# Four changes of order in a two-layer hybrid decoder trunk: pooling units swapped, state additions moved ahead of the norm, decays and an epsilon moved

## The chip, the cores and the metric

The kernel runs on one core of one Trainium2 chip. The metric is the device time of one execution in microseconds, as the median of several runs. All arithmetic is float32; large matrix products are made of two parts per operand (a high and a low one), in three passes.

## The reference, cut to what matters

A sequence of 2048 tokens with 1024 channels runs through two layers. Layer 0 has one input projection that feeds gated linear attention (4 heads, chunks of 64, with a low-rank, data-dependent forget gate) and a spatial-gating MLP. Layer 1 has one input projection that feeds retention (4 heads, rotary positions) and a causal pooling mixer of widths 2, 4, 8 and 16. In both layers each branch is multiplied by a SiLU gate, the branches are concatenated and projected back, and x becomes LayerNorm(alpha * x + y). The parts that the change touches:

```python
# layer 0, the forget gate
log_a = log_sigmoid(a_lr @ w_a2 + b_a) / 16          # a_lr: 16 columns of the input projection
b = cumsum(log_a)  # within chunks of 64
q_dec, k_dec = q * exp(b), k * exp(-b)
...
# both layers, chunkwise: state entering each chunk
S[n] = decay[n-1] * S[n-1] + U[n-1]
o = o_intra + q_dec @ S
o_a = rmsnorm(o) * silu(g_a)         # layer 1: groupnorm(o) * silu(g_c)
...
# layer 1, pooling: group g of 128 channels has width w = (2, 4, 8, 16)[g]
outs[g] = mean of the last w tokens - p[g]
o_d = (outs[g] @ w_pool[g]) * scale * silu(g_d)
...
y = concat([o_c, o_d]) @ w_out
x = layer_norm(alpha * x + y)                        # (x - mu) * rsqrt(var + eps) * g + b
```

## The kernel before, in words

**Tiling and order.** The 2048 tokens are worked in 4 blocks of 512; each block goes through both layers before the next. Every projection is a *unit* (`unit`, L164): 512 output columns or rows, as 4 tiles of 128, each summed over 8 k-tiles in 3 passes of a 128x512 matmul on TensorE. With `width=2` a unit is two halves of two tiles, 48 matmuls per half. The order of instructions is written by hand: each engine runs its own in the order in which the program issues them. There is no planner.

**Steps.** What isn't a projection is cut into steps that are put between chunks of a unit. `later(fn, delay)` (L144) appends a step; `between()` (L147) counts each step's delay down by one and runs those that reach zero, in the order in which they were appended. With `width=2`, `between()` is called in the middle of each half (after 4 of 8 k-tiles) and after the half's results have been handed to `evac`: four times a unit. A step that `evac` appends with a delay of 1 runs in the same half's closing `between()`. `flush()` (L158) runs everything that is left.

**Weights.** They stream in 256 KB loads on SP's queue (`fetch`, L102) in the order of `stream`, whose groups follow `ORDER` (L33), into a ring of 7 raw buffers. `cut` (L114) splits one into a high part (a ScalarE copy, L89) and a low part (a VectorE subtraction, L90) in a ring of 12 slots. `pace` (L124) issues cuts while a unit runs, as slots come free: eight in each second half, in steady state.

**PSUM.** Projections take 4 banks (`big`), attention 2 (`att`, L389), and transposes, chunk states, pooling products and decay products share 2 banks (`tr`, L77, tile name `trp`).

**Layer 0's gate.** The first unit of a layer gives half of the values and the 16 low-rank columns. `low_rank` transposes these (L511) into `alrT` (L512), `decay` calls `gla_decay` (products L455; Abs, Exp and Ln on ScalarE, L458 to L464), and `decay2` calls `gla_exps` (cumulative sum on VectorE, L471 to L478; exponentials on ScalarE, L482 to L485). They are steps of the second values unit, whose chunks are half as long (256 columns). The unit of queries and keys follows; when its first half ends, `evac_qk` multiplies by the exponentials into G (L549, L550), and `state_keys` transposes G two steps later (L555).

**Attention.** `attend` (L378) serves both layers. It appends `first` and four `outputs(t)`, one per tile of 128 tokens. `outputs(t)` issues the output products of tile t (L385, into the two `att` banks), then the scores and the chunk states of tile t+1 (into both `tr` banks), then `norm` (statistics, and the POOL's `rstd`), then `prepare` of tile t+1 (masked copies of the scores, L413; four state additions, L417, which read the `tr` banks; the state's decay, L733 in layer 1), and last the scaling, L752 in layer 1, which frees the `att` banks.

**Layer 1's units.** They are, in this order: queries and keys, values, `pool_unit(1)` (widths 8 and 16), the gates of retention, `pool_unit(0)` (widths 2 and 4), and then the output projection with its layer norm. The delays (3, 4, 5, 7, 9) put `first` in the middle of the second half of the values unit, outputs(0) at its end, outputs(1) and outputs(2) in the middles of the two halves of the first pooling unit, and outputs(3) in the middle of the first half of the unit behind it. A pooling unit's first half gives two groups of p: copies into `pb` (L786), then `sums`: shifted additions on VectorE (L793; 1, 2, 3 and 4 of them for widths 2, 4, 8 and 16), a small POOL correction in block 0 alone (L796), the mean minus identity (L798) and the split into `cd`. Its second half gives two SiLU gates (L773), and then `out` multiplies by the pooling weights (products L778, 3 per group, into a `tr` bank) and by the gate (`gate`, L206), whose result is split into the same place of `cd` (L207). `slot = (g + 2) % 4` places the groups, so the output projection takes widths 8 and 16 as k-tiles 4 and 5 and widths 2 and 4 as 6 and 7.

**Layer norm.** `layer_norm_out` (L209) adds the residual (L219), takes statistics (L220, L223), lets `rstd` (L192) form (var + eps) ** -0.5 on the POOL in two instructions (L198 the sum, L201 the power), while the VectorE runs the first normalising pass (L228); the second pass (L231) waits for the POOL. `rstd` with a float epsilon and a scale of 1 is used here and in layer 0's spatial gating (L608).

Of the kernel before, what the change touches and what calls it, by code (L numbers as in the profile page):

```python
# [13 lines left out]
ALU = mybir.AluOpType  # L14
# [15 lines left out]
SLOTS = 12  # L30


ORDER = [0, 1, 2, 3, 4, 5, 6, 7, 8, 11, 9, 10, 12, 13]  # L33


def _parts(value, bits, n):
# [15 lines left out]
def trunk(ctx, tc, x, xT, pos, wv, w, w_a2, pvec, rowp, sgu_rows, w_sT, w_pool, ropec, poolc, out):  # L52
    nc = tc.nc
# [23 lines left out]
    def tr():  # L77
        return ps_tr.tile([P, 4, P], F32, tag="tr", name="trp")

    def w2(name):  # L80
        return work.tile([P, TB], F32, tag="w2", name=name)

    def flat(t):
        return t.rearrange("p a b -> p (a b)")


    def split(src, hi, lo):

        nc.scalar.activation(hi, src, AF.Copy)  # L89
        nc.vector.tensor_tensor(lo, src, hi.bitcast(F32), op=ALU.subtract)  # L90
# [4 lines left out]
    for b in range(NB):  # L95
        stream += [(wv[kt, :, 0:272],) for kt in range(KT)]
        stream += [(wv[kt, :, 272:528], wv[kt + 1, :, 272:528]) for kt in range(0, KT, 2)]
        stream += [(w[g, kt],) for g in ORDER for kt in range(KT)]
    landed, ready, small_loads = [], [], []
# [44 lines left out]
    def later(fn, delay=1):  # L144
        steps.append([delay, fn])
# [12 lines left out]
    def flush():  # L158
        while steps:
            between()  # L160
# [31 lines left out]
    def rstd(dst, var, eps, scale=1.0):  # L192

        n = dst.shape[1]
        if not isinstance(eps, float):
            nc.gpsimd.tensor_tensor(dst, var, eps, op=ALU.add)
        elif scale == 1.0:
            nc.gpsimd.tensor_scalar(dst, var, eps, None, op0=ALU.add)  # L198
        else:
            nc.gpsimd.tensor_scalar(dst, var, scale, eps, op0=ALU.mult, op1=ALU.add)  # L200
        nc.gpsimd.tensor_tensor(dst, dst, neghalf[:, :n], op=ALU.pow)  # L201

    def gate(dst_u, h, psT, gain, sil):

        y = w2("y")
        nc.vector.scalar_tensor_tensor(y, psT, gain, sil, op0=ALU.mult, op1=ALU.mult)  # L206
        later(lambda: split(y, dst_u[:, h, 0, :], dst_u[:, h, 1, :]))  # L207
# [55 lines left out]
    s_mid = const.tile([P, 2, P], F32, name="s_mid")  # L263
# [24 lines left out]
    for kt in range(KT):  # L288
# [4 lines left out]
        t = wpool.tile([P, 2, 512], F32R, tag="w", name="wt")  # L293
# [64 lines left out]
    def half(n):  # L358
        return slice(64 * n, 64 * n + 64)
# [18 lines left out]
    def attend(qk, kt, vt, state, upd, norm, delays):  # L378

        states = [state, s_odd]

        def mm(dst, lhsT, rhs, start=False, stop=False):
            nc.tensor.matmul(dst, lhsT=lhsT, rhs=rhs, start=start, stop=stop, skip_group_check=True)  # L385

        def banks():

            return [ps_s.tile([P, 4, P], F32, tag="s", name="att") for _ in range(2)]  # L389

        def vals(t, s, r, c):
            return vt(t)[half(r), (2 * c + s) * P:(2 * c + s + 1) * P]

        def scores(t, ps, start):
            for c in range(2):
                for s in range(2):
                    for r in range(2):
                        k, q = qk(s, 64 * r, t)
                        mm(ps[r][half(r), 2 + c, half(s)], k[:, half(c)], q[:, half(c)],
                           start=start and c == 0 and s == 0, stop=True)  # L400

        def chunk_states(t):
            u = [tr(), tr()]
            for s in range(2):
                for c in range(2):
                    for r in range(2):
                        mm(u[r][half(c), s, :], kt(s, r, c, t), vals(t, s, r, c), start=s == 0, stop=True)
            return u

        def prepare(t, ps, u):  # L410
            after = states[(t + 1) % 2]
            for r in range(2):
                nc.vector.copy_predicated(pm[t % 2][half(r)], mask_b[half(r)],  # L413
                                          ps[r][half(r), 2:4, :].rearrange("p c (s i) -> p (c s) i", i=64))
            for dst, src, c in ((s_mid, states[t % 2], 0), (after, s_mid, 1)):
                for r in range(2):
                    nc.vector.tensor_tensor(dst[half(r)], src[half(r)], u[r][half(c), 0:2, :], op=ALU.add)  # L417
            upd(t, after)

        def first():  # L420
            ps = banks()
            scores(0, ps, True)
            prepare(0, ps, chunk_states(0))

        def outputs(t):
            m, ps = pm[t % 2], banks()
            last = t == NT - 1
            for s in range(2):
                for c in range(2):
                    for r in range(2):  # L430
                        mm(ps[r][half(c), s, :], m[half(r), 2 * c + s, :], vals(t, s, r, c), start=s == 0)
            for s in range(2):
                for c in range(2):
                    for r in range(2):
                        mm(ps[r][half(c), s, :], qk(s, 64 * r, t)[1][:, half(c)],
                           (states[t % 2], s_mid)[c][half(r), s, :], stop=True)
            if not last:
                scores(t + 1, ps, False)
                u = chunk_states(t + 1)
            scale = norm(t, [p_[:, 0:2, :] for p_ in ps])  # L440
            if not last:
                prepare(t + 1, ps, u)
            scale()

        later(first, delays[0])
        for t in range(NT):
            later(lambda t=t: outputs(t), delays[t + 1])
# [40 lines left out]
    def layer0(b, xs):  # L488
# [6 lines left out]
        def values(t, ps, s):  # L495
            by_heads(both_copy if b == 0 and s == 0 else act_copy,
                     lambda r, c: vt[half(r), t, (2 * c + s) * P:(2 * c + s + 1) * P],
                     lambda c, r: ps[half(c), r * P:(r + 1) * P])
# [31 lines left out]
            later(constants2, 3)  # L530
            later(constants3, 4)
        later(low_rank, 2)
        later(decay, 3)
        later(decay2, 4)
        unit(xs, lambda t, ps: values(t, ps, 1), True, cols=256)


# [124 lines left out]
        for i in range(2):  # L662
            r = r8.tile([P, 2, D], F32, tag="r8", name="rows")
# [23 lines left out]
    def layer1(b, xs, rows):  # L687
# [44 lines left out]
        def upd(t, st):  # L732
            nc.vector.tensor_tensor(st, st, g128.unsqueeze(2).broadcast_to([P, 2, P]), op=ALU.mult)  # L733
# [33 lines left out]
        def pool_unit(half):  # L767
            def evac(n, ps):
                g = 2 * half + n % 2
                slot = (g + 2) % 4  # L770
                if n >= 2:
                    sg = w2("sg")
                    nc.scalar.activation(sg, ps, AF.Silu)  # L773

                    def out():
                        pt = flat(tr())
                        for n, (i, j) in enumerate(PASSES):
                            nc.tensor.matmul(pt, lhsT=wp[:, i, g * P:(g + 1) * P], rhs=cd[:, slot, j, :],  # L778
                                             start=(n == 0), stop=(n == 2))
                        gate(cd, slot, pt, pool_s[:, g:g + 1], sg)  # L780

                    later(out, 1)
                    return
                pb = pl.tile([P, 16 + TB], F32, tag="pl", name="pb")
                nc.vector.tensor_copy(pb[:, 0:16], carry[:, g, :])
                nc.scalar.activation(pb[:, 16:], ps, AF.Copy)  # L786

                def sums():
                    src, off, step = pb, 0, 1
                    while step < WINDOWS[g]:  # L790
                        off2 = off + step
                        dst = pl.tile([P, 16 + TB], F32, tag="pl", name="pl")
                        nc.vector.tensor_tensor(dst[:, off2:], src[:, off2:], src[:, off2 - step:16 + TB - step], op=ALU.add)  # L793
                        src, off, step = dst, off2, step * 2
                    if b == 0:
                        nc.gpsimd.tensor_tensor(src[:, 16:32], src[:, 16:32], poolt[:, g, :], op=ALU.mult)  # L796
                    pd = w2("pd")
                    nc.vector.scalar_tensor_tensor(pd, src[:, 16:], 1.0 / WINDOWS[g], pb[:, 16:],  # L798
                                                   op0=ALU.mult, op1=ALU.subtract)
                    if b < NB - 1:  # L800
                        nc.vector.tensor_copy(carry[:, g, :], pb[:, TB:TB + 16])

                    split(pd, cd[:, slot, 0, :], cd[:, slot, 1, :])

                later(sums)

            unit(xs, evac, False)

        pool_unit(1)

        def evac_gc(h, ps):
            sg = w2("sg")
# [8 lines left out]
            later(out, 1)  # L821

        unit(xs, evac_gc, False)
        pool_unit(0)
        flush()
        load_x(b + 1)

# [21 lines left out]
    for b in range(NB):  # L849
        x1, rows = layer0(b, list(xunits))  # L850
        layer1(b, x1, rows)
# [68 lines left out]
```

## Time and profile before

| | |
|---|---|
| median of 3 runs | 1496.98 us (1495.4 to 1497.81) |
| the profiled execution's own time | 1497.93 us |
| its span, from the first to the last instruction | 1496.2 us |
| TensorE matmuls | 1468.6 us busy (98%), 8752 of them |
| VectorE | 983.5 us (66%) |
| ScalarE (ACT) | 596.3 us (40%) |
| GpSimd (POOL) | 115.9 us (8%) |
| mean granted TensorE clock | 0.994 of full speed |
| DMA | 162.35 MB, mean 109 GB/s |

PE is TensorE's matmuls and PEld its weight loads, DVE is VectorE, ACT is ScalarE, POOL is GpSimd, SP issues the DMAs. The time lies 1.7 us above the span, for what stands around it. Matmuls are pipelined, so that the busy share of TensorE says little of how near it is to its peak; its waits and its granted clock say where time is lost. Idle time of the other engines costs nothing unless TensorE, or the end of the program, waits for them.

### The profile page before, as it was taken

What the parts mean: (1) busy time and instruction counts of PE and PEld (TensorE: products, weight loads), DVE (VectorE), ACT (ScalarE), POOL (GpSimd) and SP (SyncE); (2) the same over time, 40 slices, a digit from 0 to 9 for tenths busy, and PEclk for the clock granted to TensorE, in tenths of its full rate; (3) what the DMA queues carried; (4) which work ended last, traced back from release to release, by engine and by line L of the source; (5) the groups of instructions that cost most, each with busy time, mean ns of one, the idle gap of its engine ahead of it and who ended that gap; (6) DMA issues with size and microseconds to landing.
All of it is one profiled execution on the core that took longest, in us unless ns stands there. A gap on an engine that the chain in (4) does not pass through costs nothing.

```text
span 1496.2 us, 23299 instructions
## 1 busy us (share of the span) xinstructions
PE 1468.6 (98%) x8752; PEld 1225.9 (82%) x8752; DVE 983.5 (66%) x2008; ACT 596.3 (40%) x1116; POOL 115.9 (8%) x185
## 2 busy tenths in 40 slices
PE   8999999999999999999999999999999999999997
PEld 7788888788988888878898888887888888888786
DVE  5596586756657458676665746867576664696755
ACT  6534324243653333434274342333427434143430
POOL 1020010000101001000100100000010010100002
PEclk9999999999999999999999999999999999999999
DMA  7324423124523341313452343232435325222321
GB/s 231 106 85 141 134 64 114 57 67 161 184 71 108 120 141 57 114 57 110 131 183 78 93 139 115 59 111 64 144 103 171 92 79 170 84 92 79 97 80 57
DMA packets 87058, 162.35 MB, mean 109 GB/s; under 512 B 10096, under 2 KB 18336, under 8 KB 86944
## 3 DMA queue, kind: packets, MB, share of 16 engines
q1 hardware_dynamic: 86944, 160.85, 34.6%
q8 instruction: 69, 1.13, 0.3%
q14 instruction: 45, 0.37, 0.1%
HBM read 152.43 MB, written 8.39 MB: 107 GB/s over the span
## 4 chain that ended last, share of the span: by engine, by line
PE 93%; DVE 4%; ACT 1%; DMA 1%; issue 1%; POOL 0%; DVEq 0%; POOLq 0%; ACTq 0%; SPq 0%
PE big L181 84%; PE att L385 3%; DVE pl L793 1%; PE trp L778 1%; PE trp L626 1%; PE trp L678 1%; PE trp L385 1%; DVE wt L90 1%; PE trp L818 0%; PE trp L653 0%; PE trp L718 0%; DMA raw<-in_wv 0%; DMA xraw<-in_xT 0%; ACT T L89 0%; DVE pd L798 0%
## 5 line engine op out<-in xcount | busy, mean ns | idle before, releaser
L181 PE MATMUL big<-wt,T 128*128 128x512 f32 (+2 forms) x3456 | 726.0, 369 | 7.2 <-ACT wt L89 4.5
L181 PEld LDWEIGHTS big<-wt,T 128*128 128x128 f32 x3456 | 599.0, 189 | 114.2 <-ACT wt L89 4.5
L181 PE MATMUL big<-T,wt 128*128 128x512 f32 x2688 | 629.7, 393 | 0.8 <-ACT wt L89 0.8
L181 PEld LDWEIGHTS big<-T,wt 128*128 128x128 f32 x2688 | 502.4, 189 | 109.5 <-issue 4.8
L90 DVE TENSOR_TENSOR wt<-raw,wt 128x512 fp32r<-128x512 f32 (+1 forms) x496 | 317.3, 672 | 247.5 <-ACT wt L89 246.9
L89 ACT ACTIVATE wt<-raw 128x512 fp32r<-128x512 f32 (+1 forms) x496 | 296.7, 616 | 329.0 <-PE big L181 256.4
L219 DVE SCALAR_TENSOR_TENSOR rows<-rows,big 128x512 f32<-128x512 f32 x64 | 43.6, 681 | 59.3 <-PE big L181 59.3
L198 POOL TENSOR_SCALAR lnrs<-lnmv 128x1 f32<-128x1 f32 x32 | 33.3, 1042 | 616.1 <-DVE lnmv L223 616.1
L370 ACT ACTIVATE v<-big 64x128 f32<-64x128 f32 (+1 forms) x184 | 56.7, 308 | 36.0 <-PE big L181 19.0
L680 ACT ACTIVATE T<-trp 128x512 fp32r<-128x512 f32 x32 | 17.4, 596 | 105.7 <-PE trp L678 105.7
L231 DVE SCALAR_TENSOR_TENSOR rows<-rows,lnrs,ln 128x1024 f32<-128x1024 f32 (+1 forms) x36 | 41.6, 1166 | 19.5 <-POOL lnrs L201 18.6
L201 POOL TENSOR_TENSOR rs<-rs,neghalf 128x4 f32<-128x4 f32 x48 | 49.3, 1028 | 3.9
L220 DVE BATCH_NORM_STATS2 lnst<-rows 128x6 f32<-128x512 f32 x64 | 44.4, 694 | 2.2
L228 DVE SCALAR_TENSOR_TENSOR rows<-rows,lnmv,ln 128x1024 f32<-128x1024 f32 x32 | 41.0, 1282 | 0.9
L206 DVE SCALAR_TENSOR_TENSOR y<-trp,pv,sg 128x512 f32<-128x512 f32 x48 | 33.7, 744 | 9.5 <-PE trp L653 5.3
L786 ACT ACTIVATE pb<-big 128x512 f32<-128x512 f32 x16 | 9.6, 598 | 75.0 <-PE big L181 74.5
L638 ACT ACTIVATE act<-big 128x512 f32<-128x512 f32 x32 | 18.3, 597 | 51.2 <-PE big L181 50.5
L89 ACT ACTIVATE T<-y 128x512 fp32r<-128x512 f32 x48 | 29.4, 627 | 22.2 <-DVE y L206 21.8
L604 DVE BATCH_NORM_STATS2 st<-zt 128x6 f32<-128x128 f32 x64 | 13.7, 276 | 35.1 <-ACT zt L600 35.1
L90 DVE TENSOR_TENSOR T<-y,T 128x512 fp32r<-128x512 f32 x48 | 31.7, 689 | 0.5
L793 DVE TENSOR_TENSOR pl<-pb 128x527 f32<-128x527 f32 x16 | 11.3, 704 | 31.2 <-ACT pb L786 31.2
L744 DVE BATCH_NORM_STATS2 st<-att 128x6 f32<-128x128 f32 x64 | 14.2, 284 | 22.5 <-PE att L385 22.0
(197 smaller groups left out, 978.6 us busy)
## 6 DMA issues: line engine op xcount, KB each, us to landing
raw<-in_w SPq DMA_DIRECT2D x448, 256.0 KB, 3.0
xraw<-in_xT SPq DMA_DIRECT2D x32, 256.0 KB, 3.5
rows<-in_x SPq DMA_DIRECT2D x8, 1024.0 KB, 7.2
ln<-in_rowp SPq DMA_DIRECT2D x16, 512.0 KB, 6.1
out<-rows SPq DMA_DIRECT2D x12, 512.0 KB, 2.7
raw<-in_wv SPq DMA_DIRECT2D x32, 136.0 KB, 3.3
raw<-in_wv SPq DMA_DIRECT2D x32, 128.0 KB, 2.9
out<-rows SPq DMA_DIRECT2D x8, 256.0 KB, 2.0
```

Of the source, the lines that this page charges most:

```text
L89: nc.scalar.activation(hi, src, AF.Copy)
L90: nc.vector.tensor_tensor(lo, src, hi.bitcast(F32), op=ALU.subtract)
L181: nc.tensor.matmul(p_, lhsT=lhsT, rhs=rhs, start=(kt == 0 and q == 0), stop=(kt == KT - 1 and q == 2))
L198: nc.gpsimd.tensor_scalar(dst, var, eps, None, op0=ALU.add)
L201: nc.gpsimd.tensor_tensor(dst, dst, neghalf[:, :n], op=ALU.pow)
L206: nc.vector.scalar_tensor_tensor(y, psT, gain, sil, op0=ALU.mult, op1=ALU.mult)
L219: nc.vector.scalar_tensor_tensor(rh, rh, ALPHA, ps, op0=ALU.mult, op1=ALU.add)
L220: nc.vector.bn_stats(sts[t][:, half, :], rh)
L228: nc.vector.scalar_tensor_tensor(row, row, mv[:, 0:1], gt, op0=ALU.subtract, op1=ALU.mult)
L231: nc.vector.scalar_tensor_tensor(row[:, cs], row[:, cs], rs, bt[:, cs], op0=ALU.mult, op1=ALU.add)
L370: nc.scalar.activation(dst, src, AF.Copy)
L385: nc.tensor.matmul(dst, lhsT=lhsT, rhs=rhs, start=start, stop=stop, skip_group_check=True)
```

## The change

Five edits. The pooling units swap places: widths 2 and 4 come first, beside the attention, and widths 8 and 16 behind the retention gates; `ORDER` follows. The pooling products of the first of them get a delay of 2 instead of 1 (the second keeps 1). In `attend`, the four state additions leave `prepare` for a function of their own, which `outputs` calls right behind the chunk states' products, ahead of the norm. `decay` and `decay2` each run a step later. The epsilon of `rstd` is added on VectorE where it is a float and the scale is 1. The places of the groups in `cd` stay.

```diff
-ORDER = [0, 1, 2, 3, 4, 5, 6, 7, 8, 11, 9, 10, 12, 13]
+ORDER = [0, 1, 2, 3, 4, 5, 6, 7, 8, 10, 9, 11, 12, 13]
...
         elif scale == 1.0:
-            nc.gpsimd.tensor_scalar(dst, var, eps, None, op0=ALU.add)
+            nc.vector.tensor_scalar(dst, var, eps, None, op0=ALU.add)
...
-        def prepare(t, ps, u):
+        def carry_on(t, u):
             after = states[(t + 1) % 2]
+            for dst, src, c in ((s_mid, states[t % 2], 0), (after, s_mid, 1)):
+                for r in range(2):
+                    nc.vector.tensor_tensor(dst[half(r)], src[half(r)], u[r][half(c), 0:2, :], op=ALU.add)
+
+        def prepare(t, ps):
             for r in range(2):
                 nc.vector.copy_predicated(pm[t % 2][half(r)], mask_b[half(r)],
                                           ps[r][half(r), 2:4, :].rearrange("p c (s i) -> p (c s) i", i=64))
-            for dst, src, c in ((s_mid, states[t % 2], 0), (after, s_mid, 1)):
-                for r in range(2):
-                    nc.vector.tensor_tensor(dst[half(r)], src[half(r)], u[r][half(c), 0:2, :], op=ALU.add)
-            upd(t, after)
+            upd(t, states[(t + 1) % 2])
 
         def first():
             ps = banks()
             scores(0, ps, True)
-            prepare(0, ps, chunk_states(0))
+            carry_on(0, chunk_states(0))
+            prepare(0, ps)
...
             if not last:
                 scores(t + 1, ps, False)
-                u = chunk_states(t + 1)
+                carry_on(t + 1, chunk_states(t + 1))
             scale = norm(t, [p_[:, 0:2, :] for p_ in ps])
             if not last:
-                prepare(t + 1, ps, u)
+                prepare(t + 1, ps)
             scale()
...
         later(low_rank, 2)
-        later(decay, 3)
-        later(decay2, 4)
+        later(decay, 4)
+        later(decay2, 5)
...
-                    later(out, 1)
+                    later(out, 2 - half)
...
-        pool_unit(1)
+        pool_unit(0)
...
         unit(xs, evac_gc, False)
-        pool_unit(0)
+        pool_unit(1)
```

## Rows read from the trace of the kernel before

**Rows 1.** Waits of TensorE over the whole span: total, times, longest.

```profile
PE trp L778 <- DVE s L417: 8.4, 4, 2.5
PE big L181 <- ACT wt L89: 5.3, 2, 4.5
PE trp L455 <- ACT alrT L512: 3.1, 3, 1.0
```

**Rows 2.** Timeline, block 0, first pooling unit: start, length; in brackets idle before, releaser.

```profile
287.54 2.10 PE L778 MATMUL trp<-T,wp 128*128 128x512 f32 x6 [2.54 <-DVE s L417]
```

**Rows 3.** TensorE by stretches: from, to, length, busy, clock, DMA share, GB/s.

```profile
404.52:408.15 3.63, 3.63 (x26) 1.00 0.48 132
...
287.54:296.24 8.70, 8.70 (x34) 0.80 0.43 126
...
1025.76:1034.43 8.67, 8.67 (x34) 0.80 0.39 121
1394.85:1401.94 7.09, 7.09 (x34) 1.00 0.41 127
337.45:344.31 6.86, 6.86 (x32) 1.00 0.91 324
```

**Rows 4.** Timeline, block 0, pooling chains of the first and the last unit.

```profile
271.32 1.28 ACT L786 ACTIVATE pb<-big 128x512 f32<-128x512 f32 x2 [10.86 <-PE big L181]
...
281.10 0.69 DVE L90 TENSOR_TENSOR T<-pd,T 128x512 fp32r<-128x512 f32 x1 [0.61 <-ACT T L89]
...
325.98 1.22 ACT L786 ACTIVATE pb<-big 128x512 f32<-128x512 f32 x2 [7.79 <-PE big L181]
...
332.88 0.69 DVE L90 TENSOR_TENSOR T<-pd,T 128x512 fp32r<-128x512 f32 x1 [0.61 <-ACT T L89]
...
340.40 1.35 DVE L90 TENSOR_TENSOR T<-y,T 128x512 fp32r<-128x512 f32 x2
```

**Rows 5.** Timeline, block 1, the decays of layer 0.

```profile
405.41 1.24 ACT L458 ACTIVATE ta<-trp,pv 128x512 f32<-128x512 f32 x2
...
410.43 1.15 ACT L464 ACTIVATE ta<-ta 128x512 f32<-128x512 f32 x2
...
412.53 2.25 ACT L370 ACTIVATE v<-big 64x128 f32<-64x128 f32 x8
...
413.35 0.68 DVE L471 TENSOR_TENSOR tb<-tb,ta 128x512 f32<-128x512 f32 x1
...
420.28 0.68 DVE L549 TENSOR_TENSOR G<-big,ta 128x512 f32<-128x512 f32 x1
...
424.51 0.60 PE L555 MATMUL trp<-ident,G 128*128 128x128 f32 x4
```

**Rows 6.** Timeline, block 0, layer 1, from outputs(0) to outputs(1).

```profile
256.69 0.67 PE L385 MATMUL att<-v,pm 64*64 64x128 f32 x16
...
258.08 0.62 PE L385 MATMUL trp<-v,ks 64*64 64x128 f32 x14
258.28 0.89 DVE L744 BATCH_NORM_STATS2 st<-att 128x6 f32<-128x128 f32 x4
...
259.81 1.01 POOL L201 TENSOR_TENSOR rs<-rs,neghalf 128x4 f32<-128x4 f32 x1
...
262.52 1.37 DVE L752 TENSOR_SCALAR v<-att,mv,rs 128x128 f32<-128x128 f32 x4
...
264.29 0.67 PE L385 MATMUL att<-v,pm 64*64 64x128 f32 x16
```

**Rows 7.** Timeline, the last layer norm of the program.

```profile
1489.84 1.28 DVE L228 SCALAR_TENSOR_TENSOR rows<-rows,lnmv,ln 128x1024 f32<-128x1024 f32 x1
...
1491.89 1.42 DVE L231 SCALAR_TENSOR_TENSOR rows<-rows,lnrs,ln 128x512 f32<-128x512 f32 x2 [0.77 <-POOL lnrs L201]
...
1489.89 1.31 POOL L198 TENSOR_SCALAR lnrs<-lnmv 128x1 f32<-128x1 f32 x1 [3.48 <-DVE lnmv L223]
```

**Rows 8.** One line's instructions, L198: count, shortest, median and longest in ns, starts.

```profile
L198 POOL TENSOR_SCALAR lnrs<-lnmv x32: 221/1312/1324, 191.9 to 1489.9; 128x1 f32<-128x1 f32 x32
```

## The prediction

> **What bounds the kernel now.** TensorE does, and nearly without a pause. I read first the list of what TensorE waited for over the span [rows 1]: its largest entry is L778, the pooling products, with 8.4 us in four waits, one per block of 512 tokens, all released by the state addition of L417; L455, the decay products, waits three times for alrT, 3.1 us together. (The ACT weight entry, 5.3 us, is 4.5 at the start and 0.8 in block 0.) Other engines count only where they make TensorE wait, and in steady state these two lines are the only places.
>
> The timeline shows what L778 waits for [rows 2]. Its operands are long ready; it needs a `tr` bank, of which there are two, and both hold the chunk states of outputs(2), which the VectorE adds to the state. Those adds stand behind everything the VectorE had queued: seven shifted additions of widths 8 and 16 and their splits, then weight splits, then the norm statistics and the masked copies.
>
> The granted clock by stretches [rows 3] shows a second price. After the wait, the six products and the 24 matmuls behind them take 8.70 us in block 0 at a clock of 0.80; the same work in the last pooling unit, without a wait, takes 6.86 us at 1.00. Block 2 takes 8.67 (block 1 reads alike), block 3 takes 7.09. Behind the L455 wait, the first row of [rows 3], the clock stays at 1.00, so there the wait is all.
>
> **The change part by part.**
>
> *Pooling and state additions.* Products of widths 2 and 4 move from the end of their unit to the middle of the next half unit, behind outputs(3), which takes no `tr` bank. By then (a chunk of 5.5 us later) the adds have long run: they now stand ahead of the norm, and the shifted additions ahead of them are three instead of seven. The pooling chain from the first copy to the last split is 281.79 - 271.32 = 10.47 us with widths 8 and 16, and 333.57 - 325.98 = 7.59 with 2 and 4 [rows 4], 2.9 us shorter. So the whole wait goes, 8.4 us, and with it the clock loss: 8.70 - 6.86 = 1.84, twice that or so again (1.81 in block 2, block 1 taken between), and 7.09 - 6.86 = 0.23; together 5.7 us.
>
> What may be late next is the last unit before the output projection, which gets the longer chain. Products there need the fourth split 10.5 us after the first copy and come at 337.45 - 325.98 = 11.5: 1.0 us to spare. Then the gate results. Today the last low part is done at 340.40 + 1.35 = 341.75 [rows 4]; moved by 2.9 it is 344.63, the one before it, now k-tile 4 of the projection, about 343.95. k-tile 4 begins at 344.31, where the last row of [rows 3] ends, and reads its low half in the third pass, 0.45 later: 0.8 us to spare. I take nothing here; bounds 0 and +6 us (a wait of about 1.5 in each of four blocks). The reordered weights are the same 256 KB loads in the same queue places: SP's queue issues as many DMAs, each a split later by at most those 2.9 us, and weights are cut at least four k-tiles ahead (some 5.5 us). Nothing.
>
> *Adds first, in layer 1.* This has a price. Outputs(0) and outputs(1) are 264.29 - 256.69 = 7.60 us apart, and outputs(1) needs the banks that the scaling of outputs(0) releases at 262.52 + 1.37 = 263.89: a margin of 0.40 [rows 6]. Now the VectorE starts with adds that need the chunk states (done at 258.70) instead of statistics that start at 258.28: 0.45 later, so the scaling would end at 264.35. Beyond that, the POOL's answer had 262.52 - 260.82 = 1.70 us to spare while four adds ran behind the statistics; these now run ahead of them, and the spare is about gone. So TensorE waits some 0.1 to 0.3 us, and I take 0.4 per block for hand-overs between engines: 1.6 us over four blocks; bounds 0 and 2.8. Waits of 1.0 us left the clock alone [rows 3]. In layer 0 steps are further apart, and nothing is lost.
>
> *Decays.* L455 moves from the middle to the end of a chunk that lasts 3.63 - 0.66 = 2.97 us (the first row of [rows 3], less two products that now start the next one), long after alrT: the three waits go, 3.1 us, with no gain in the clock. But the rest starts later. TensorE reaches the end at 403.50 + 2.97 = 406.47. ACT then has a weight split (0.6) and eight value copies, 2.25 us, which used to follow the decays [rows 5], so Abs starts near 409.3 instead of 405.41, and the first Ln result, 5.65 us behind Abs today (410.43 + 0.63), comes at 414.95. The scan chain started at 413.35 and G followed at 420.28, 6.93 later: now 421.9, ready at 422.6. Its first user is the transpose at 424.51, which also comes 1.0 earlier, 423.5. It is hidden, with 0.9 us left of 3.5. I take nothing; bounds 0 and +3 us (three blocks, 1 us each). Block 0 had no L455 wait. There L455 shares its step with the constants' product, so its second bank is free only after an addition (up to +1), but a weight split now comes ahead of the decay chain, which should end the 0.8 us wait [rows 1]. I take zero; bounds -0.8 and +1.
>
> *Epsilon.* At the end of the program the chain is statistics, POOL addition, POOL power, last VectorE pass. The addition takes 1.31 us [rows 7] though the same instruction can take 0.22 [rows 8]: it lasts until the 1.28 us VectorE pass beside it ends (1489.84 + 1.28 = 1491.12). Moved to the VectorE it costs some 0.1 (an estimate, no more than the POOL's shortest 0.22), but now the power starts under that pass and is probably held the same way: ready near 1491.6 instead of 1491.86. I take 0.25 gained; bounds 0.1 (held in full) and 0.65 (not held; then the first pass sets the start). Earlier normalisations and the 16 of layer 0 end behind no TensorE wait: nothing.
>
> Sum: 8.4 + 5.7 + 3.1 + 0.25 - 1.6 = 15.85. The profiled execution took 1497.93 us (a span of 1496.2), so it would take 1482.1; it lies 0.95 above the median of 1496.98, from which I get **1481.1 us**.
>
> **Rivals.**
>
> *The wait moves to the projection* (ends slower). The four parts of widths 8 and 16 finish right ahead of the projection. If the gate chain runs later than worked out, TensorE waits at k-tile 4, and a wait of some 2 us also costs clock, 1.84 [rows 3]. Per block 15.85 / 4 - 1.84 = 2.1 us is the point from which all is given back, that is, splits 2.9 us later than I have them. At 3 us of wait: 4 x 4.84 = 19.4, less 15.85, about 1500.5. For it: ACT and VectorE are both blocked for some 10 us by the pooling chain and then owe eight weight splits. Against it: no attention step stands in that unit, and the same chain ended in time in the first unit. Chance 0.04; a partial wait (1484.5 to 1493) 0.08.
>
> *Decays late.* If the chain through three table loads slips by over 0.9 us, the transposes wait: 1 to 3 us in three blocks, so 1484 to 1490. Its operations are all in the rows, only their new order isn't. Chance 0.09.
>
> *The POOL holds the VectorE.* In outputs(0) the state's decay (L733) now meets the POOL's power. If VectorE instructions that read two operands from SBUF stand still while the 1.01 us power [rows 6] runs, L733, which would have run under it, runs behind it. The scaling then starts later by L733's own length, under half a microsecond, the next product waits about 0.7 per block instead of 0.4, and the result is 1482.3. The Trainium skill, SBUF — State Buffer, section "SBUF: two separate sides", says so: VectorE and GpSimd share a port pair as an exclusive lock, and whoever comes second blocks. The trace shows the other direction, the POOL held by the VectorE [rows 7, 8]; no row here shows the VectorE held. Chance 0.15.
>
> *It doesn't do what it says.* If something else held the products (a bank for another reason), the waits would stay under another name, and only 3.3 less 1.6 would be won: 1495.2; with the decays late also, 1497. Against it: all four waits name the same releaser. Chance 0.04.
>
> **How the numbers follow.** The forecast holds 0.60; it and the POOL rival lie between 1479 and 1484. The low end: no attention wait, 0.65 at the end, block 0 winning 0.8, which is 1496.98 - 18.65 = 1478.3. The high end takes in late decays and the smaller partial waits, 1488; what is left out is the upper half of the partial wait and the last cases, under 2 in 10 with what may lie below. A measurement of this kernel can tell about 0.2% from no change, 3 us. All but the slower case and the no-effect case are faster by more: 0.92 faster, 0.04 same, 0.04 slower.
>
> **What would show it.** L778 should vanish from TensorE's waits, the 30 matmuls behind each first pooling unit should run at 1.00, L455 should wait nowhere in blocks 1 to 3. An L385 wait of 0.1 to 0.7 us on L752 in layer 1 would confirm the price. The G split's distance to L555 should shrink to about 1 us. The prediction is wrong if waits of over 1 us appear at L181 behind the second pooling unit, or at L555.

## The result and the profile after

The changed kernel takes 1480.69 us (median, 1480.44 to 1480.94), beside 1497.39 us for the kernel before in the same comparison: a ratio of 0.9889, 95% interval 0.9872 to 0.9907, so 1.1% faster. The forecast was 1481.1. The span fell from 1496.2 to 1479.0 us, by 17.2, and the mean granted clock rose from 0.994 to 0.997.

What TensorE waits for after the change (line, releaser: total, times, longest) is all at the start and in block 0:

```profile
PE big L181 <- ACT wt L89: 4.5, 1, 4.5
PE big L181 <- DVE v L373: 2.1, 2, 1.1
PE trp L458 <- DVE cst L325: 0.4, 1, 0.4
PE big L181 <- DVE wt L90: 0.2, 1, 0.2
```

Beside [rows 1], the pooling products (now L781) are gone with their 8.4 us, and the decay products (now L458) have lost their three waits and gained one of 0.4 in block 0.

Two rows of the timeline of block 0, after (start, length): the last state addition in the first pooling unit, and that unit's products, now in the middle of the next half unit.

```profile
281.78 0.86 DVE L414 TENSOR_TENSOR s<-s_mid,trp 64x256 f32<-64x256 f32 x2
...
290.79 1.66 PE L781 MATMUL trp<-T,wp 128*128 128x512 f32 x6
```

The last state addition, which frees the banks, ends at 282.64; the products come at 290.79, over 8 us later, and nothing holds them, unlike in [rows 2]. The stretch behind them, to be read beside [rows 3] (from, to, length, busy, clock, DMA share, GB/s), is 1.7 us shorter at full clock:

```profile
290.79:297.75 6.96, 6.96 (x34) 1.00 0.16 55
```

The last pooling unit, now with widths 8 and 16, answers to [rows 4]:

```profile
320.85 1.28 ACT L789 ACTIVATE pb<-big 128x512 f32<-128x512 f32 x2 [7.73 <-PE big L181]
...
330.69 0.69 DVE L90 TENSOR_TENSOR T<-pd,T 128x512 fp32r<-128x512 f32 x1 [0.61 <-ACT T L89]
...
332.22 1.56 PE L781 MATMUL trp<-T,wp 128*128 128x512 f32 x6
333.62 12.67 PE L181 MATMUL big<-wt,T 128*128 128x512 f32 x55
...
337.56 1.35 DVE L90 TENSOR_TENSOR T<-y,T 128x512 fp32r<-128x512 f32 x2
```

The chain lasts 331.38 - 320.85 = 10.5 us, and its products start 0.8 us behind its end. The projection runs through from 333.62 without a wait.

The decays of block 1, beside [rows 5]:

```profile
401.24 0.72 PE L458 MATMUL trp<-alrT,wa 48*128 48x512 f32 x2
...
416.87 0.68 DVE L552 TENSOR_TENSOR G<-big,ta 128x512 f32<-128x512 f32 x1
...
418.34 0.60 PE L558 MATMUL trp<-ident,G 128*128 128x128 f32 x4
```

G is ready at 417.55 and transposed at 418.34: the cover has shrunk to 0.8 us, as worked out, and holds.

Outputs(0) to outputs(1) in layer 1 of block 0, beside [rows 6], is where the price is:

```profile
257.57 5.73 PE L181 MATMUL big<-T,wt 128*128 128x512 f32 x24
...
257.69 0.86 DVE L414 TENSOR_TENSOR s_mid<-s_odd,trp 64x256 f32<-64x256 f32 x2 [0.60 <-PE trp L385]
...
261.12 1.01 POOL L201 TENSOR_TENSOR rs<-rs,neghalf 128x4 f32<-128x4 f32 x1
...
261.56 0.42 DVE L736 TENSOR_TENSOR s<-s,rope 128x256 f32<-128x256 f32 x1
262.17 1.36 DVE L755 TENSOR_SCALAR v<-att,mv,rs 128x128 f32<-128x128 f32 x4 [0.19 <-POOL rs L201]
263.36 0.87 PE L385 MATMUL att<-v,pm 64*64 64x128 f32 x13
263.97 0.27 PE L385 MATMUL att<-s_odd,qkT 64*64 64x128 f32 x1
264.03 0.31 PE L385 MATMUL att<-v,pm 64*64 64x128 f32 x3
...
265.61 11.17 PE L181 MATMUL big<-T,wt 128*128 128x512 f32 x48
```

The VectorE starts with the additions and waits for the chunk states, and the scaling waits 0.19 us for the POOL and ends at 263.53, when the output products have already begun. They come in two pieces, 13 and 3, with others between. From one chunk's start to the next it is 265.61 - 257.57 = 8.04 us, 0.44 more than the 7.60 of before.

Last, the end of the program, beside [rows 7]; first the power in the kernel before, then the changed kernel:

```profile
1491.29 0.57 POOL L201 TENSOR_TENSOR lnrs<-lnrs,neghalf 128x1 f32<-128x1 f32 x1
...
1472.62 0.21 DVE L223 BATCH_NORM_AGGREGATE lnmv<-lnst 128x2 f32<-128x12 f32 x1
1472.87 0.16 DVE L198 TENSOR_SCALAR lnrs<-lnmv 128x1 f32<-128x1 f32 x1
1472.94 1.28 DVE L228 SCALAR_TENSOR_TENSOR rows<-rows,lnmv,ln 128x1024 f32<-128x1024 f32 x1
1474.65 1.41 DVE L231 SCALAR_TENSOR_TENSOR rows<-rows,lnrs,ln 128x512 f32<-128x512 f32 x2 [0.44 <-POOL lnrs L201]
...
1473.10 1.51 POOL L201 TENSOR_TENSOR lnrs<-lnrs,neghalf 128x1 f32<-128x1 f32 x1 [3.93 <-DVE lnrs L198]
```

The power, 0.57 us in the trace before, now lasts 1.51 us: until the pass beside it ends (1474.22), and 0.4 more.

**Where the 17.2 us came from.** TensorE's own marks cut both traces into stages that hold the same work: from the low-rank transposes to the first transposes of G, and from the last rotary transposes to the products of the second pooling unit (differences of their start times, in us).

```
stage                            block    before   after    won
low rank to G                      0       25.74   24.89   0.85
low rank to G                  1, 2, 3     24.48   23.39   1.09 each
rotary to second pooling products  0       93.31   89.30   4.01
                                   1       92.72   89.30   3.42
                                   2       92.69   89.30   3.39
                                   3       91.12   89.30   1.82
aggregate to the last pass         3        2.30    2.03   0.27
start, to the first transposes     0       29.06   28.85   0.21
```

The sum is 17.2 us. All other stages are equal to a few hundredths. The start is a matter of the execution: TensorE's clock was granted at 0.50, the lower of its two levels (1.2 GHz), for a stretch near 23 us in some traces and not in others, and the low-rank transposes come at 28.69 to 29.06 us in the five traces where it was and at 27.91 to 28.52 in the seven where it wasn't.

### The profile page after: what moved, and what is told of

It reads as the page before. It is cut to its first block, busy times and chain, and to the rows that moved or that the text cites. A ratio compares the mean times of both kernels' runs of the same rounds, so it can differ in the third digit from the quotient of the medians.

```text
span 1479.0 us, 23323 instructions
## 1 busy us (share of the span) xinstructions
PE 1463.8 (99%) x8752; PEld 1224.1 (83%) x8752; DVE 989.7 (67%) x2056; ACT 595.6 (40%) x1116; POOL 101.0 (7%) x137
## 4 chain that ended last, share of the span: by engine, by line
PE 98%; issue 0%; DVE 0%; DMA 0%; ACT 0%; POOLq 0%; POOL 0%; DVEq 0%; ACTq 0%
PE big L181 89%; PE att L385 3%; PE trp L385 1%; PE trp L629 1%; PE trp L681 1%; PE trp L781 1%; PE trp L656 0%; PE trp L821 0%; PE trp L721 0%; PE trp L558 0%; DMA xraw<-in_xT 0%; PE trp L458 0%; PE trp L514 0%; POOLq L919 0%; POOL lnrs L201 0%
## 5 line engine op out<-in xcount | busy, mean ns | idle before, releaser
L181 PE MATMUL big<-wt,T 128*128 128x512 f32 (+2 forms) x3456 | 725.2, 369 | 6.7 <-ACT wt L89 4.5
L181 PEld LDWEIGHTS big<-wt,T 128*128 128x128 f32 x3456 | 599.1, 190 | 112.3 <-ACT wt L89 4.5
L181 PE MATMUL big<-T,wt 128*128 128x512 f32 x2688 | 625.7, 391 | 0.0
L181 PEld LDWEIGHTS big<-T,wt 128*128 128x128 f32 x2688 | 500.6, 188 | 107.7 <-issue 5.4
L201 POOL TENSOR_TENSOR lnrs<-lnrs,neghalf 128x1 f32<-128x1 f32 x32 | 40.8, 1275 | 628.0 <-DVE lnrs L198 628.0
L90 DVE TENSOR_TENSOR T<-xraw,T 128x512 fp32r<-128x512 f32 x32 | 21.2, 685 | 13.3 <-ACT T L89 13.3
```

The source lines that it names most:

```text
L181: nc.tensor.matmul(p_, lhsT=lhsT, rhs=rhs, start=(kt == 0 and q == 0), stop=(kt == KT - 1 and q == 2))
```

## The experiments

All times are compared with the kernel before on the same chip.

**The swap alone.**

```diff
-ORDER = [0, 1, 2, 3, 4, 5, 6, 7, 8, 11, 9, 10, 12, 13]
+ORDER = [0, 1, 2, 3, 4, 5, 6, 7, 8, 10, 9, 11, 12, 13]
-        pool_unit(1)
+        pool_unit(0)
...
-        pool_unit(0)
+        pool_unit(1)
```

> The swap of the two pooling units alone, products still right behind their unit. Theory (the bank wait is a backlog of the VectorE): the shifted additions ahead of the state additions are 2.9 us shorter, TensorE waited 2.5 us in block 0 and 2.0 in the others, so L778 waits 0 to 0.1 us, the matmuls behind it run at a clock of 1.00, and the time falls by 8.4 + 5.7 = 14.1 us, to about 1483.3. Rival (the later products are what removes the wait): L778 still waits over 1 us per block and the clock falls; 1490 to 1497. Rival (the long pooling chain costs in its new place): new L181 waits behind the second pooling unit, with the clock down; over 1488.

1483.52 against 1497.31 us, ratio 0.9911 (0.9896 to 0.9926). L778 is not among the waits of TensorE, and no L181 wait appears behind the second pooling unit; the decay waits are still there:

```profile
PE big L181 <- ACT wt L89: 5.3, 2, 4.5
PE trp L455 <- ACT alrT L512: 3.1, 3, 1.1
```

The products and the 24 matmuls behind them, the stretch of [rows 3], now run without a wait and at full clock:

```profile
284.07:291.11 7.04, 7.04 (x35) 1.00 0.42 142
```

So 2.9 us less of shifted additions is enough by itself: the wait was a backlog of the VectorE.

**The additions first, alone.**

```diff
-                u = chunk_states(t + 1)
+                carry_on(t + 1, chunk_states(t + 1))
             scale = norm(t, [p_[:, 0:2, :] for p_ in ps])
             if not last:
-                prepare(t + 1, ps, u)
+                prepare(t + 1, ps)
```

> The state additions first alone. Theory: the statistics, their aggregates and the masked copies, 2.0 us together, no longer stand ahead of the additions, so the L778 wait is about 0.6 us in block 0 and 0 in the others, with a clock of 1.00 behind it: -7.8 and -5.7 us. Outputs(1) in layer 1 waits as in the changed kernel, 0.44 us per block: +1.8. Sum -11.7: about 1485.7. Rival (the wait is set by the shifted additions and the weight splits alone): waits of over 1 us stay, 1490 or more.

1487.71 against 1497.31 us, ratio 0.9939 (0.9924 to 0.9954), 2 us above the expectation. The products' rows in blocks 0 and 1 (blocks 2 and 3 are as block 1):

```profile
285.14 1.65 PE L781 MATMUL trp<-T,wp 128*128 128x512 f32 x6 [0.83 <-DVE s L414]
...
651.43 1.63 PE L781 MATMUL trp<-T,wp 128*128 128x512 f32 x6 [0.23 <-DVE s L414]
```

The waits are 1.5 us together where 0.6 was expected: I had the additions done a quarter of a microsecond too soon. The rest is a smaller thing. From the rotary to the second pooling unit's products block 1 takes 89.87 us, 0.91 more than with the swap alone (88.96); 0.44 of that is the price at outputs(1) and 0.23 the wait, which leaves 0.24. A short wait costs more than its own length. The direction held, and the rival that kept waits of over 1 us did not.

**The later products alone** (the first unit still has widths 8 and 16).

```diff
-                    later(out, 1)
+                    later(out, 1 + half)
```

> The products of the first pooling unit (here still widths 8 and 16) one chunk later, alone. Theory: the banks are free long before, no L778 wait, clock 1.00: -14.1 us, about 1483.3. So each of the three edits would do nearly alone what the three do together. Rival (the wait moves on): the gates then hold the banks, and the transposes of the retention gates (L818) or outputs(3) wait 1 to 2 us per block: 1488 to 1492.

1483.25 against 1497.31 us, ratio 0.9909 (0.9894 to 0.9924). The only waits past the start and block 0 are L455's 3.1 us, and the retention gates' transposes don't wait. Each of the three edits alone removes the wait or most of it. Together they win no more than one: 88.86 us from the rotary transposes to the second pooling unit's products in this run, and 89.30 in the changed kernel.

**A longer wait** (the statistics of outputs(2) in layer 1 are taken twice).

```diff
+            if t == 2:
+                spare = small.tile([P, 4, 6], F32, tag="spare", name="spare")
+                for h in range(4):
+                    nc.vector.bn_stats(spare[:, h, :], o[h % 2][:, h // 2, :])
```

> The kernel before with the statistics of outputs(2) in layer 1 taken twice (the second set is not used), so the L778 wait is 0.9 us longer in each block: 3.4, 2.9, 2.9, 2.9. Theory (a wait costs its length, and the clock loss behind it is a price of its own that does not grow with it): +3.6 us for the waits, with the loss of 1.8 us in blocks 0 to 2 as before: about 1501. Rival (the clock loss grows with the wait, or block 3, which lost only 0.23, now loses as much as the others): +5 to +8, 1502.5 to 1505. Rival (TensorE is not really held by the VectorE): no change, 1497.4.

1501.33 against 1497.31 us, ratio 1.0028 (1.0017 to 1.0038): 4.0 us, nearer to the theory's 3.6, though the interval, 2.5 to 5.7 us, reaches into the first rival's 5 to 8. But the stretches behind the waits say that its clause on the clock was wrong. The waits were 3.35 us in block 0 and about 2.74 in the others. (In these three the profile names ScalarE's SiLU, L777, as the releaser. But in all four blocks the first product starts 0.14 or 0.15 us behind the third state addition, as it does in the kernel before; the first SiLU ends 0.1 us ahead of it in these three, 0.7 in block 0, and behind its start in the kernel before.) Columns as in [rows 3]; a clock of 0.80 is the mean over a stretch of the two levels, 1.00 and 0.50 (2.4 and 1.2 GHz):

```profile
288.01:296.66 8.65, 8.65 (x34) 0.80 0.41 122
657.78:664.87 7.09, 7.09 (x34) 1.00 0.41 129
1026.01:1035.96 9.95, 9.95 (x34) 0.69 0.34 105
1397.08:1405.75 8.67, 8.67 (x34) 0.80 0.36 123
```

Against the 7.04 us of the swap alone, block 0 loses 1.6 us, block 1 next to nothing at full clock, block 2 loses 2.9, and block 3, which was spared before, 1.6. The loss is neither a constant nor a function of the wait's length alone: the same wait of 2.74 us cost 0, 2.9 and 1.6 us. What decides it in a given block stays open.

**The decays alone.**

```diff
-        later(decay, 3)
-        later(decay2, 4)
+        later(decay, 4)
+        later(decay2, 5)
```

> The decays a step later, alone. Theory: the three waits at the decay products go, 3.1 us (1.09 per block in the trace of the changed kernel), and block 0 wins 0.8 because a weight split comes ahead of the decay chain: about -4.1, 1493.3. The transposes of G do not wait; the multiplication by the exponentials ends 0.7 to 0.9 us ahead of them in blocks 1 to 3. Rival (block 0 won for another reason, as the start varies from run to run): -3.3, with the 0.8 us wait of block 0 still there.

1492.85 against 1497.15 us, ratio 0.9972 (0.9962 to 0.9982): 4.3 us, near the theory's 4.1, but the interval, 2.7 to 5.7 us, holds the rival's 3.3 too, so the trace has to decide. In the waits, ACT's entry has lost its second wait, that of block 0, and the constants' one has come; L778 is untouched:

```profile
PE trp L778 <- DVE s L417: 8.4, 4, 2.5
PE big L181 <- ACT wt L89: 4.4, 1, 4.4
...
PE trp L455 <- DVE cst L325: 0.4, 1, 0.4
```

Block 0 takes 24.90 us from the low-rank transposes to those of G, as in the changed kernel (24.89), against 25.74 before and 25.73 in the run with the swap alone. The start of this stage varied by 1 us from run to run, but with the decays in the same place its length stayed within a few hundredths, so block 0's 0.85 belongs to this edit.

**The epsilon alone.**

```diff
-            nc.gpsimd.tensor_scalar(dst, var, eps, None, op0=ALU.add)
+            nc.vector.tensor_scalar(dst, var, eps, None, op0=ALU.add)
```

> The epsilon on the VectorE, alone. Theory (the POOL's power is held by the VectorE pass beside it): the last pass starts 0.2 to 0.3 us sooner behind the aggregate, nothing else moves: 1497.0, not to be told from no change. Rival (the power runs beside the pass): 0.65 us sooner at the end.

1496.14 against 1497.07 us, ratio 0.9992 (0.9982 to 1.0003): not to be told from no change by its times. At the end the aggregate starts at 1484.17 and the last pass at 1486.19, 2.02 us later, against 2.30 before: 0.28, the theory's case. But "nothing else moves" was wrong. The decay products' entry among TensorE's waits has halved:

```profile
PE trp L455 <- ACT alrT L512: 1.5, 3, 0.5
```

The timeline ahead of it, first of this run, then of the kernel before (block 1):

```profile
386.49 1.28 DVE L231 SCALAR_TENSOR_TENSOR rows<-rows,lnrs,ln 128x1024 f32<-128x1024 f32 x1 [0.44 <-POOL lnrs L201]
...
389.50 0.17 DVE L502 CAST alr<-big 128x16 fp32r<-128x16 f32 x1
...
389.95 2.27 ACT L370 ACTIVATE v<-big 64x128 f32<-64x128 f32 x8 [2.12 <-DVE alr L504]
```

```profile
387.70 1.28 DVE L231 SCALAR_TENSOR_TENSOR rows<-rows,lnrs,ln 128x1024 f32<-128x1024 f32 x1 [0.77 <-POOL lnrs L201]
...
390.71 0.17 DVE L502 CAST alr<-big 128x16 fp32r<-128x16 f32 x1
...
391.17 2.27 ACT L370 ACTIVATE v<-big 64x128 f32<-64x128 f32 x8 [2.46 <-DVE alr L504]
```

The last layer norm of a block still occupies the VectorE when the next block begins: behind its last pass stand three weight splits and the copies of the low-rank columns, behind these ACT's value copies, and behind those, in turn, `alrT`. The pass now waits 0.44 instead of 0.77 us for the POOL, twice in a row, and blocks 1 to 3 each take 23.95 us from the low-rank transposes to those of G instead of 24.48. The edit is worth 0.28 + 3 x 0.53 = 1.9 us alone, of which the medians show 0.9, within their scatter. With the decays moved, the same 1.6 us are won by the move already.

The scatter shows in the clock. Of this kernel's twelve executions the two shortest (1491.46 and 1492.23 us) have a mean granted clock of 0.997, and the five longest (1497.74 to 1498.13) 0.992 or 0.993. The span of this execution is 1490.5 us, 5.7 under that of before. The four stretches behind the L778 waits, which last 2.54 and three times 1.95 us as before, are 3.2 us shorter together than those of [rows 3]:

```profile
286.98:295.57 8.59, 8.59 (x34) 0.81 0.39 129
655.45:662.56 7.11, 7.11 (x34) 1.00 0.45 141
1022.43:1029.53 7.10, 7.10 (x34) 1.00 0.44 114
1389.40:1396.51 7.11, 7.11 (x34) 1.00 0.40 125
```

The clock fell behind one wait here, and behind three in [rows 3]. The fall itself, seen from close by in block 0 of the kernel before: the clock is still granted in full for 0.9 us behind the wait, and then stands at the lower level.

```profile
288.60:291.80 3.20, 3.20 (x9) 0.50 0.16 17
```

Single times of this kernel lie between 1491.5 and 1498.1 us; those of the changed kernel, which has no such waits, lie within 0.5 us.

**The changed kernel without early additions** (`prepare` and `outputs` as before; all else as changed).

```diff
-                carry_on(t + 1, chunk_states(t + 1))
+                u = chunk_states(t + 1)
             scale = norm(t, [p_[:, 0:2, :] for p_ in ps])
             if not last:
-                prepare(t + 1, ps)
+                prepare(t + 1, ps, u)
```

> The changed kernel with the state additions put back behind the norm; all other edits stay. Theory: with the pooling units swapped and the products later nothing needs the additions early, and the wait of outputs(1) in layer 1 goes: 4 x 0.44 = 1.8 us less than the changed kernel, about 1478.9 where that has 1480.7. Rival (the early additions carry part of the gain): L781 or outputs(3) waits again, 1482 or more.

**The changed kernel again**, in the same comparison.

> The changed kernel again, beside the others on one chip: 1480.7, waits of 0.44 us per block at outputs(1) in layer 1.

1478.65 and 1480.85 us (ratios 0.9879, 0.9864 to 0.9894, and 0.9893, 0.9879 to 0.9906; single times 1478.52 to 1479.18 and 1480.71 to 1481.02). Undoing this one part makes it 2.2 us faster. Every block takes 88.86 us from the rotary transposes to the second pooling unit's products, 0.44 less than 89.30: four times that is 1.8, and the rest lies at the start and in block 0: in the trace of the changed kernel the clock stood at 0.50 from 22.60 to 25.90 us, in this one it was full there, ahead of anything that the edit touches. So the early additions, once the other two edits stand, cost 1.8 us and win nothing.

**That, and two small edits more.**

```diff
-            later(constants3, 4)
+            later(constants3, 6)
...
-                    nc.vector.scalar_tensor_tensor(row, row, mv[:, 0:1], gt, op0=ALU.subtract, op1=ALU.mult)
+                    for c in range(0, D, D // cuts):
+                        cs = slice(c, c + D // cuts)
+                        nc.vector.scalar_tensor_tensor(row[:, cs], row[:, cs], mv[:, 0:1], gt[:, cs],
+                                                       op0=ALU.subtract, op1=ALU.mult)
```

> As the run without early additions, and two small edits more: in block 0 the product of the constants two steps later, so that the decay product there finds a free bank (0.35 us), and in the last layer norm the first normalising pass in two halves, so that the POOL's power can start between them. If the POOL is held by that pass for its whole length, the power ends 0.4 us sooner: together about 1478.2. If it is not held by the pass, only 0.35: 1478.6 or a little above, for the extra instruction.

1477.96 us, ratio 0.9873 (0.9860 to 0.9887), the fastest of all. The end of its program:

```profile
1470.19 0.21 DVE L223 BATCH_NORM_AGGREGATE lnmv<-lnst 128x2 f32<-128x12 f32 x1
...
1470.50 1.40 DVE L230 SCALAR_TENSOR_TENSOR rows<-rows,lnmv,ln 128x512 f32<-128x512 f32 x2
1471.82 1.41 DVE L234 SCALAR_TENSOR_TENSOR rows<-rows,lnrs,ln 128x512 f32<-128x512 f32 x2
...
1470.66 0.98 POOL L201 TENSOR_TENSOR lnrs<-lnrs,neghalf 128x1 f32<-128x1 f32 x1 [4.46 <-DVE lnrs L198]
```

With the pass in halves the power lasts 0.98 us instead of 1.51 and ends before the second half does, so that the last pass no longer waits for it. It starts 1.63 us behind the aggregate instead of 2.03: 0.4, as expected if the POOL is held by a pass until its end. The constants' wait is gone too (24.59 us to G instead of 24.92).

**The gates of the last unit delayed**, to see how near the projection is to waiting.

```diff
+                        if half == 1:
+                            spare = small.tile([P, 2, 6], F32, tag="spare", name="spare")
+                            for i in range(2):
+                                nc.vector.bn_stats(spare[:, i, :], sg)
                         gate(cd, slot, pt, pool_s[:, g:g + 1], sg)
```

> The changed kernel with four needless statistics of 0.7 us (their results are not used) ahead of the gates of widths 8 and 16, which are the last work before the output projection: the four splits end 2.8 us later. Theory (in the trace of the changed kernel the first low part is done 1.3 us before the projection's fifth k-tile reads it): TensorE waits 1.2 to 1.5 us at L181 in each block, plus some 0.2 us to start again, so 1486.5 to 1488 if the clock holds; if it falls behind these waits as it did behind those of 2 us, up to 1495. Rival (the projection has more room than that, or the VectorE's order does not set it): under 1482.

1483.14 us, ratio 0.9907 (0.9893 to 0.9922): between the two expectations. TensorE now waits where the first rival of the prediction put it:

```profile
PE big L181 <- DVE T L90: 1.3, 4, 0.8
```

The wait is 0.8 us in block 0 and 0.15 in the others, and from these pooling products to the next block's low-rank transposes (in block 3, to the end) block 0 takes 1.15 us longer than the changed kernel and the others 0.46: 2.5 us in all. The wait is smaller than expected for two reasons: the first low part, on which the k-tile waits, came 2.2 us later behind the products and not 2.8, and blocks 1 to 3, which have no POOL correction in their pooling chain, have some 0.7 us more room. The place and the mechanism of the rival are real; the clock held behind these short waits.

## Why the prediction was right

**The pooling products.** 8.4 us of waits and 5.7 of clock, less 1.6 for outputs(1), are 12.5; the four blocks won 4.01 + 3.42 + 3.39 + 1.82 = 12.6. The step that read the wait as a backlog of the VectorE was confirmed by the swap alone, by the additions alone and, the other way, by the longer statistics; the later products alone show that the wait was for the bank. The sum of 14.1 us met the 14.0 that these stages won by the swap alone, but in part by luck. The same work without a wait was counted as 6.86 us from 337.45, but the products of that unit start ahead of that:

```profile
337.29 1.56 PE L778 MATMUL trp<-T,wp 128*128 128x512 f32 x6
```

So the 6.86 is some 0.2 us short; the stretch takes 7.04 with the swap alone. Against this the four stretches of before (8.70, 8.69, 8.67 and 7.09) lost 5.0 us to the clock and not 5.7. The other 0.6, some 0.16 per block, was lost around the waits beyond the length that the list gives them. Nor is the clock's loss a fixed price: it falls on some waits and not on others. In an execution like the epsilon run's the same step would have given 3.2 us less, which is why such a sum has to be put against its own execution's time first.

**What may be late next.** Nothing was. The chain of widths 8 and 16 ended 0.8 us ahead of its products where I had 1.0; counted to 337.29 it would have been 0.8. The first low half came 1.3 us ahead of its k-tile, where I had 0.8: done at 338.24, while the third pass of that k-tile is 5.46 + 0.45 behind 333.62. The delayed gates show that this cover is thin but real.

**The additions first.** The term was 0.4 us per block and measured 0.44, and the reason was the one given: the VectorE begins later, and the POOL's answer is no longer covered (0.19 us). The L385 wait on L752 that I had named as the sign of it did not appear: TensorE's list of waits shows nothing of this price, and the stage lengths do.

**The decays.** 3.1 us were worked out and 3 x 1.09 = 3.3 measured. In block 0 I took zero and it won 0.85, a mis-sized term, just past its lower bound of -0.8. The addition that its second bank waits for cost 0.4 and not up to 1. The 72 matmuls around the wait of 0.8 that ended took 54.80 - 36.89 = 17.9 us, and 53.74 - 37.31 = 16.4 after: 1.5 less, of which the wait itself is 0.8. Where the rest comes from is not shown.

**The epsilon.** 0.25 at the end against 0.27 measured. The POOL is held by the VectorE pass, as the power's 1.51 us and, in halves, 0.98 us show. One sentence of the step was wrong: "Earlier normalisations and the 16 of layer 0 end behind no TensorE wait". Those at a block's end stand at the head of the chain to `alrT`, and alone they would have taken half of the L455 wait. It made no difference to the sum, as the moved decays cover the same wait.

**The rivals.** Decays late: the cover came out at 0.8 us and held. The POOL holding the VectorE: the row at 261.56 decides it. L736 has two operands in SBUF, starts in the middle of the power (261.12 to 262.13) and takes its usual 0.42 us. In all twelve places of this trace where it meets the power it takes 0.42 or 0.43. So the exclusive lock of the Trainium skill, SBUF — State Buffer, section "SBUF: two separate sides", is borne out here only in one direction: the POOL waited for the VectorE, and the VectorE did not wait for the POOL. By that section's wording L736 would have ended about 0.6 us later. The profile's spans on the POOL are rough, so when in its span the power reads SBUF is not shown.

## What to carry to other kernels

When the bound engine waits for a buffer, look in the releasing engine's queue for what stands ahead of the instruction that frees it; shortening that, moving the release forward and asking later are three cures for one wait, and the cheapest one should be used alone, since here the third turned into a price of 0.44 us per block. Read what a wait costs from the length of a whole stage between two marks of the bound engine: the list of waits left out the loss of clock behind long waits, some 0.1 to 0.3 us of starting again behind short ones, and one new wait altogether. Before a long chain is moved, work out its cover at the new place in time units, since that number, here 0.8 to 1.3 us, is what the next edit may spend.

## What the runs showed of the hardware that was not expected

What makes the clock fall behind a wait is not settled by these traces: with the same waits of 1.95 us it fell in two blocks of three in one execution and in none of three in another, a wait of 2.74 us cost between nothing and 2.9 us, and in the run with the decays alone the wait of 2.54 us in block 0 cost no clock (1.00 in the stretch behind it) while two of 1.95 did (0.80). Behind the single waits of about 1.0 us or less in the blocks it fell nowhere; at the start of the changed kernel it did fall to 0.50 behind two waits of 1.01 and 1.10 us that lie 0.6 us apart. The kernels without the long waits are also the steadier ones: 0.2 to 1.1 us between the lowest and highest of four times, against 3.4 for the kernel before.

A POOL instruction of 0.2 to 0.6 us that meets the 1.28 us VectorE pass with two SBUF operands lasts until that pass ends and a little longer, 0.1 us for the addition (1.31 us in all) and 0.4 for the power (1.51). Beside the VectorE's splits L684, which read one operand from PSUM and one from SBUF, the same power took its normal length (0.54 us, eight times in the trace of the changed kernel, as at 201.87). The VectorE held by the POOL was not seen.
